# Projecting the mLSTM's values with tokens on partitions, two heads at a time

## The chip, the cores and the metric

One core of a Trainium2 chip runs the whole kernel in one launch. TensorE (PE) multiplies matrices, VectorE (DVE), ScalarE (ACT) and GpSimd (POOL) work on elements, and DMA queues move data, issued here by SyncE (SP). The metric is the device time of one execution in microseconds (us): the median of several runs, 1819.1 us for the kernel before.

## The reference, cut to what matters

One layer of a streaming trunk: a prompt of 1024 tokens and eight requests of 16 tokens share the weights, so 1152 token rows go through each product. The layer is a mixer, an attention into 256 memory tokens, and a feed-forward block. The mixer projects the normalised input once, by `w_in`, and splits the columns between four mLSTM heads and four gated-delta (gdn) heads, each 128 wide:

```
proj = xn @ w_in                       # 1024 -> q,k,v,o of 4 mLSTM heads, gates, q,k,v,z of 4 gdn heads
s    = einsum('bhtd,bhsd->bhts', q, k) * w_intra                  # mLSTM: weights within a chunk
num  = w_inter * einsum('bhtk,bhkv->bhtv', q, C0) + einsum('bhts,bhsv->bhtv', s, v)
den  = w_inter * einsum('bhtk,bhk->bht', q, n0) + sum(s, -1)
h    = num / maximum(abs(den), exp(-m))
C1   = decay0 * C0 + einsum('bhs,bhsk,bhsv->bhkv', w_s, k, v)     # the state carried to the next chunk
```

The queries and keys of an mLSTM head enter `s` with features on the contracted axis. Its values `v` enter only sums over tokens (`s @ v`, `k^T v`), where tokens are contracted.

## The kernel before, in words

**Products.** All data is float32. For a projection each operand is split into a high and a low fp32r half (`xh`, `xl`, `wh`, `wl`), and a product is three matmuls (`mm3`, L233 to L235; L234 to L236 in the changed kernel). A projection chunk is one column block of 128 features: for each of three blocks of 384 tokens, eight steps over the 1024 inputs, three matmuls each, so 72 matmuls of 384 columns, with features on the partitions of the result. The weights of a chunk (128x1024) are loaded by SP, cast on ACT (`wh`, L213) and subtracted on DVE (`wl`, L214). DVE moves each result out of PSUM and scales it by the row norm.

**The stream.** `mixers()` lists the chunks in order: first the gates, then for the heads g0 m0 g1 m1 g2 m2 g3 m3 their columns (gdn: k, q, v, which go through a short convolution; mLSTM: k, q, v), and each head's output gate (`z`) two heads late. Behind them stand eight chunks of the memory tokens' keys (`mem_k`) and eight of their values, 256 columns per matmul. A small planner, `Driver`, runs while the program is written: each dense step advances its clock by a modelled TensorE time, and generators (a head's recurrence, `gdn` or `mlstm`, and `mem_in`) are written out among the dense matmuls when their delay has passed and the flags they wait for (`until`, `wait`) are set. A scheduler then may move an instruction by priority. What stands where on each engine is fixed when the kernel is built.

**A gdn head.** `gdn` loads a decay matrix `D` by DMA (L698), transposes keys and queries (`kt`, `qt`, L263) while ACT sums squares (`junk`, L728), adds masks to `D` on POOL (L703, L704), takes exponentials on ACT, and multiplies keys with keys and queries (`kq`, L755 and L756, evacuated by two DVE operations, L757 and L758). A long recurrence follows; its last product with the state is L909. `head_out` multiplies by the norm on POOL (L967, 128x1152), transposes back (`ot`, L263), applies the gate on DVE and stores.

**An mLSTM head.** `mlstm` waits for the gates, its k, q and v and for the head before it. It loads its row `R`, transposes v in nine 128x128 pieces (`vt`, L1007) with an ACT copy per three (L1008), then per token tile multiplies keys with queries (`st`, L1016), takes an exponential, and multiplies on DVE (L1018); per three tiles it transposes and weights the keys (`kt`, L1021). A loop over token tiles then forms states and outputs (`p2`, L1043; `p3`, L1050 and L1052).

**The end of the mixing stage.** `mem_in` loads the memory tokens (`mf`, L1103), splits them to `mh` (ACT, L1109) and `ml` (DVE, L1110), and forms their norms: `st` (L297), a reciprocal root, and `bc` (L284). It starts two chunks ahead of `mem_k`, once nine slots of SBUF are free; `mem_k` is written once the norms are under way.

Of the kernel before, what the change touches and what calls it, by code (L numbers as in the profile page):

```python
# [8 lines left out]
F32 = mybir.dt.float32  # L9
# [104 lines left out]
class Kern:  # L114
    def __init__(self, tc, ctx, A):
        self.tc, self.nc, self.A = tc, tc.nc, A
        mk = lambda **k: ctx.enter_context(tc.tile_pool(**k))
        self.sp = mk(name="slots", bufs=NSLOT)
        self.wp = mk(name="wts", bufs=2)
        self.cp = mk(name="consts", bufs=1)  # L120
        self.dp = mk(name="dram", bufs=1, space=bass.MemoryType.DRAM)
        self.pd = self.pm = self.pf = None
        self.n = 0
        self.live, self.held, self.reserve = 0, 0, 0
        self.dr = Driver()
# [183 lines left out]
    def consts(self):  # L309
# [44 lines left out]
    def norm_in(self, b, s, x):  # L354

        nc, v = self.nc, self.nc.vector
        add = lambda e, i, j: e.tensor_tensor(x(i), x(i), x(j), ALU.add)
        for k in range(KT):
            wc = self.prm[:, P_WMIX + k:P_WMIX + k + 1]
            xh, xl = self.xh[k][:, s], self.xl[k][:, s]  # L360
            nc.scalar.activation(xh, x(k), AF.Copy, scale=wc)
            v.scalar_tensor_tensor(xl, x(k), wc, xh, ALU.mult, ALU.subtract)
            self.done.add(f"x{b}{k}")
            yield 0.0, 0.5
        zero = 0.0
        if b == 0:
            zero = self.cp.tile([P, 1], F32, name="zero")
            v.tensor_scalar(zero, xl[:, 0:1], 0.0, None, ALU.mult)
        for k in range(KT):
            nc.scalar.activation(x(k), x(k), AF.Square, bias=zero)  # L370
            if k % 2:
                with self.hp() if b == 0 else ExitStack():
                    add(v, k - 1, k)
            yield 0.0, 0.4
        with self.hp() if b == 0 else ExitStack():
            add(v, 0, 2)
            add(v, 4, 6)
            add(v, 0, 4)
        self.F(3)
        rs = self.t(self.m1, [P, 3], "rsc", bufs=2)  # L380
        yield from self.col_stats(self.m1, x(0), 3, rs, self.rB[:, s], f"rB{b}", delay=SD if b else 2.5, spread=4.0)

    def act1(self, b):
# [274 lines left out]
    def proj_chunk(self, out, key, name):  # L658
        w = yield
        yield from self.room_s(1)  # L660
        o = self.S([P, SLOT], F32, name)

        def fin():
            out[key] = o
            self.done.add(key)

        yield from self.project(w, lambda b, ps: self.scaled(o, b, ps), fin)

    def gate_chunk(self, out, hd, last):

# [319 lines left out]
    def mlstm(self, h, r):  # L990
        nc, v, A, pool = self.nc, self.nc.vector, self.A, self.m1
        tl = lambda ap, t: ap[:, t * P:(t + 1) * P]
        self.reserve += 2
        yield from self.until("gates", f"mk{h}", f"mq{h}", f"mv{h}")
        if h:
            yield from self.until(f"mls{h - 1}")
        yield from self.room(2)
        self.reserve -= 2
        k, q, vf = r[f"mk{h}"], r[f"mq{h}"], r[f"mv{h}"]
# [5 lines left out]
        vt = vf[:, :NT * 129].rearrange("p (t d) -> p t d", d=129)  # L1005
# [970 lines left out]
    def mixers(self):  # L1976
# [5 lines left out]
        for kind, h in ORDER:  # L1982
# [3 lines left out]
                    put(base + i, self.conv_chunk(c, r))  # L1986
                body = self.gdn(h, r)
            else:
                base, hd = 16 + 4 * h, h
                for i, c in enumerate("kqv"):  # L1990
                    put(base + i, self.proj_chunk(r, f"m{c}{h}", c))
                body = self.mlstm(h, r)
            start.setdefault(len(seq), []).append((body, 1.0))
# [124 lines left out]
def _layout(x_prompt, x_sample, state_mlstm_C, state_mlstm_n, state_mlstm_m, state_gdn_S, state_gdn_conv,  # L2118
# [10 lines left out]
        cols += [s(2056 + 512), s(2056), s(2056 + 1024), s(3592)]  # L2129
    for h in range(4):  # L2130
        s = lambda o: w[:, o + h * P:o + (h + 1) * P]
        cols += [s(512), s(0), s(1024), s(1536)]
    chunk = lambda m: m.reshape(KT, P, m.shape[1] // P, P).transpose(2, 1, 0, 3).reshape(-1, P, 1024)
    prm = np.zeros((P, P_W), f)
    for o, a in ((P_WMIX, norm_mix_w[0]), (P_WX, norm_x_w[0]), (P_WMEM, norm_mem_w[0]), (P_WFFN, norm_ffn_w[0]),
# [16 lines left out]
        "xT": np.ascontiguousarray(fm(x).reshape(P, KT, NB, BW).transpose(2, 0, 1, 3)),  # L2152
        "memT": fm(mem_prompt[0]),
        "wg": np.stack([w[:, o:o + 4] for o in (2048, 2052, 4104, 4108)], 1).reshape(KT, P, 4, 4).transpose(1, 0, 2, 3),
        "win": chunk(np.concatenate(cols, axis=1)),
        "wout": chunk(w_out[0]), "wq": chunk(wq_x[0]), "wk": chunk(wk_x[0]), "wo": chunk(wo_x[0]),
        "wv": wv_x[0].reshape(2, 4, P, 4, 256).transpose(3, 0, 2, 1, 4).reshape(8, P, 1024),
# [52 lines left out]
```

## Time and profile before

| | |
|---|---|
| runs | 1816.95, 1819.1, 1823.02 us (median 1819.1) |
| profiled execution | 1822.32 us, span 1820.5 us |
| mean granted TensorE clock | 0.988 of full speed |
| busy PE, DVE, ACT, POOL | 98%, 69%, 43%, 10% |
| chain that ended last | PE 85%, DVE 7%, DMA 3%, ACT 2%, POOL 2% |

The span is what the profiler saw between the first and the last instruction; the rest of an execution's time lies around it. A busy share close to one says that PE had matmuls in hand nearly all the time, and says nothing of the pace at which they went. A window is a stretch of the span for which each engine's busy time and the granted clock are listed: where PE's busy time falls short of the stretch, PE waited; where the clock stands at 0.50, each matmul took about twice its time. In a timeline the distance from one start to the next gives the pace; the durations printed beside them overlap.

### The profile page before, as it was taken

To read this page: it belongs to the slowest core of one execution; us is meant where nothing else is said; L and a number is where in the kernel's file an instruction comes from. 1 tells how busy PE (TensorE), PEld (TensorE's weight loads), DVE (VectorE), ACT (ScalarE), POOL (GpSimd) and SP (SyncE) were. 2 spreads that over 40 slices of the span, in tenths; PEclk is the share of its full clock that TensorE was granted. 3 is DMA by queue.
4 is the path that set the end of the run, shared out by engine and by line. 5 is a ranking of instruction groups with operands and counts; after the bars stand their busy time and mean duration, and the time that the engine had idled before them with its cause. 6 is when DMAs were issued, how large, how long until landed. Compare 5 with 4: busy or idle time off the path is not lost.

```text
span 1820.5 us, 32863 instructions
## 1 busy us (share of the span) xinstructions
PE 1782.3 (98%) x13007; PEld 1728.1 (95%) x13007; DVE 1253.1 (69%) x2427; ACT 791.0 (43%) x1697; POOL 188.9 (10%) x231
## 2 busy tenths in 40 slices
PE   9999999999999999999999989999999899999997
PEld 8998899998999999988999989999999899999997
DVE  7877656765665668544677786566666888877975
ACT  6334323324315455445664444445444533433433
POOL 1124223122112202020000000000000000000003
PEclk9999999999999999999999989999999999999998
DMA  5111121121122476797154533343334843533413
GB/s 188 48 52 54 63 80 55 69 80 52 52 65 89 151 259 219 251 321 236 59 164 151 185 111 123 138 169 130 138 138 180 304 150 113 184 123 123 143 45 105
DMA packets 102258, 243.97 MB, mean 134 GB/s; under 512 B 24624, under 2 KB 50000, under 8 KB 102104
## 3 DMA queue, kind: packets, MB, share of 16 engines
q1 hardware_dynamic: 101232, 241.14, 39.2%
q8 instruction: 103, 1.69, 0.4%
q10 hardware_dynamic: 872, 0.72, 0.1%
q14 instruction: 51, 0.42, 0.1%
HBM read 183.92 MB, written 57.91 MB: 133 GB/s over the span
## 4 chain that ended last, share of the span: by engine, by line
PE 85%; DVE 7%; DMA 3%; ACT 2%; POOL 2%; issue 1%; SPq 1%; DVEq 0%; ACTq 0%; POOLq 0%
PE d L233 12%; PE d L235 11%; PE d L234 11%; PE Y L233 5%; PE Y L234 5%; PE Y L235 5%; PE Z L233 3%; PE Z L235 3%; PE Z L234 3%; PE X L235 3%; PE X L234 3%; PE X L233 3%; PE U L233 1%; PE U L235 1%; PE U L234 1%
## 5 line engine op out<-in xcount | busy, mean ns | idle before, releaser
L233 PE MATMUL d<-xh,wh 128*128 128x384 f32 x944 | 342.8, 363 | 1.1 <-DVE k L484 0.6
L235 PE MATMUL d<-xh,wl 128*128 128x384 f32 x944 | 321.4, 340 | 0.6 <-DVE wl L214 0.6
L234 PE MATMUL d<-xl,wh 128*128 128x384 f32 x944 | 318.7, 338 | 0.0
L213 ACT CAST wh<-wr 128x1024 fp32r<-128x1024 f32 x120 | 125.9, 1049 | 241.4 <-PE d L234 184.7
L214 DVE TENSOR_TENSOR wl<-wr,wh 128x1024 fp32r<-128x1024 f32 x120 | 148.7, 1239 | 76.7 <-ACT wh L213 76.4
L233 PEld LDWEIGHTS d<-xh,wh 128*128 128x128 f32 x944 | 179.7, 190 | 7.0 <-issue 5.3
L234 PEld LDWEIGHTS d<-xl,wh 128*128 128x128 f32 x944 | 179.8, 190 | 1.6 <-issue 1.4
L235 PEld LDWEIGHTS d<-xh,wl 128*128 128x128 f32 x944 | 178.7, 189 | 1.0 <-DVE wl L214 1.0
L190 ACT CAST wh<-ws 128x512 fp32r<-128x512 f32 (+3 forms) x148 | 76.2, 537 | 131.5 <-PE Y L234 73.8
L190 ACT CAST wh<-wr 128x512 fp32r<-128x512 f32 (+4 forms) x123 | 71.4, 587 | 128.2 <-PE X L234 46.0
L183 POOL TENSOR_TENSOR csy<-cst,nhalf 128x3 f32<-128x3 f32 (+2 forms) x15 | 12.6, 840 | 1005.8 <-DVE cst L276 1005.0
L233 PE MATMUL Y<-xqh,wh 128*128 128x288 f32 x336 | 99.9, 297 | 0.9 <-DVE h L1680 0.9
L191 DVE TENSOR_TENSOR wl<-ws,wh 128x512 fp32r<-128x512 f32 (+3 forms) x148 | 84.6, 585 | 22.3 <-ACT wh L190 22.1
L233 PE MATMUL Y<-hh,wh 128*128 128x288 f32 x336 | 99.2, 296 | 0.7 <-DVE E L1821 0.6
L234 PE MATMUL Y<-xql,wh 128*128 128x288 f32 x336 | 99.7, 297 | 0.0
L234 PE MATMUL Y<-hl,wh 128*128 128x288 f32 x336 | 99.2, 295 | 0.4 <-DVE hl L191 0.4
L235 PE MATMUL Y<-xqh,wl 128*128 128x288 f32 x336 | 99.6, 296 | 0.0
L235 PE MATMUL Y<-hh,wl 128*128 128x288 f32 x336 | 98.7, 295 | 0.1
L191 DVE TENSOR_TENSOR wl<-wr,wh 128x512 fp32r<-128x512 f32 (+4 forms) x123 | 79.0, 647 | 23.8 <-ACT wh L190 23.6
L190 ACT CAST hh<-ht 128x1152 fp32r<-128x1152 f32 x53 | 61.1, 1157 | 67.6 <-DMA ht<-hD 25.6
L191 DVE TENSOR_TENSOR hl<-ht,hh 128x1152 fp32r<-128x1152 f32 x53 | 71.7, 1354 | 10.2 <-ACT hh L190 10.2
L233 PE MATMUL X<-xqh,wh 128*128 128x288 f32 x224 | 66.1, 295 | 2.4 <-ACT h L1685 2.4
(496 smaller groups left out, 5220.8 us busy)
## 6 DMA issues: line engine op xcount, KB each, us to landing
ht<-hD SPq DMA_DIRECT2D x42, 576.0 KB
hD<-h SPq DMA_DIRECT2D x40, 576.0 KB
wr<-wff SPq DMA_DIRECT2D x40, 512.0 KB
wr<-win SPq DMA_DIRECT2D x32, 512.0 KB
wr<-wout SPq DMA_DIRECT2D x24, 512.0 KB
wr<-wq SPq DMA_DIRECT2D x24, 512.0 KB
wr<-wo SPq DMA_DIRECT2D x24, 512.0 KB
wr<-wd SPq DMA_DIRECT2D x32, 384.0 KB
```

Source lines behind the costliest of these rows:

```text
L183: self.nc.gpsimd.tensor_tensor(y, x, self.nhalf[:, 0:n], ALU.pow)
L190: self.nc.scalar.copy(h, x)
L191: self.nc.vector.tensor_tensor(l, x, h, ALU.subtract)
L213: nc.scalar.copy(wh, raw)
L214: (nc.gpsimd if pool else nc.vector).tensor_tensor(wl, raw, wh, ALU.subtract)
L233: mm(ps, lhsT=lh, rhs=rh, start=start, stop=False, skip_group_check=more)
L234: mm(ps, lhsT=lh, rhs=rl, start=False, stop=False, skip_group_check=more)
L235: mm(ps, lhsT=ll, rhs=rh, start=False, stop=stop, skip_group_check=more)
```

## The change

The values' columns leave the list of 128-wide chunks. A new weight array, `wvm`, holds them as 256-wide blocks (two heads side by side). `v_chunk` projects a pair of heads at once: the token tile is the stationary operand and 256 weight columns stream, so the result has tokens on partitions. Nine token tiles of 24 matmuls make 216 matmuls of 256 columns per pair. Its DVE operation scales by the row norm per token, which is now kept for all nine tiles (`rsm`, 128x9), and writes the layout that the head's loop uses. `v_load` fetches and splits the second half of a pair's weights one chunk earlier. The transposes of v and the ACT copies are removed, and `mlstm` starts with gates, k and q and waits for v only ahead of its loop. The chunk of a pair stands behind the k and q of head 0 or of head 2, so heads 1 and 3 have two chunks (k, q) where they had three, and one of the seven that stood between gdn 3's last convolution and the memory tokens' chunks is gone.

```diff
@@ act1
-        rs = self.t(self.m1, [P, 3], "rsc", bufs=2)
+        rs = self.rsm[:, 3 * b:3 * b + 3]
@@ new functions
+    def v_load(self, pair):
+        yield from self.room(3)
+        raw = self.raw_w(self.A["wvm"][2 * pair + 1], True)
+        yield 0.0, 4.0
+        self.vw[pair] = self.split_w(raw, True)
...
+    def v_chunk(self, out, pair):
+        w = yield
+        yield from self.room_s(2)
+        o = [self.S([P, SLOT], F32, "v") for _ in range(2)]
+        vt = [x[:, :NT * 129].rearrange("p (t d) -> p t d", d=129) for x in o]
+        yield from self.wait(f"vw{pair}")
+        ws = w, self.vw[pair]
+        for t0 in range(0, NT, 2):
+            n = min(2, NT - t0)
...
+            ps = self.D()
+            for j in range(n):
+                xs = slice((t0 + j) * P, (t0 + j) * P + P)
+                for k in range(KT):
+                    (wh, wl), c = ws[k // 4], slice(k % 4 * 256, k % 4 * 256 + 256)
+                    self.mm3(ps[:, j * 256:j * 256 + 256], self.xh[k][:, xs], self.xl[k][:, xs], wh[:, c], wl[:, c],
+                             k == 0, k == KT - 1)
...
+                for i in range(2):
+                    self.nc.vector.tensor_tensor(vt[i][:, t0:t0 + n, 0:P], pv[:, :, i],
+                                                 bc(self.rsm[:, t0:t0 + n], [P, n, P], 2), ALU.mult)
...
@@ mlstm
-        yield from self.until("gates", f"mk{h}", f"mq{h}", f"mv{h}")
+        yield from self.until("gates", f"mk{h}", f"mq{h}")
...
-        for g in (2, 1, 0):
-            pv = self.tr3("vt", lambda t: tl(vf, t), g)
-            nc.scalar.copy(vt[:, 3 * g:3 * g + 3, 0:P], pv)
-            yield 0.33, 0.4
-        nc.gpsimd.memset(vt[:, :, P:P + 1], 1.0)
-        yield 0.0, 0.5
...
-        num = vt
+        yield from self.until(f"mv{h}")
+        vt = num = r[f"mv{h}"][:, :NT * 129].rearrange("p (t d) -> p t d", d=129)
+        nc.gpsimd.memset(vt[:, :, P:P + 1], 1.0)
+        yield 0.0, 0.5
@@ mixers
-                base, hd = 16 + 4 * h, h
-                for i, c in enumerate("kqv"):
+                base, hd = 16 + 3 * h, h
+                body = self.mlstm(h, r)
+                for i, c in enumerate("kq"):
                     put(base + i, self.proj_chunk(r, f"m{c}{h}", c))
...
+                if h % 2 == 0:
+                    start.setdefault(len(seq) - 1, []).append((self.v_load(h // 2), 0.0))
+                    start.setdefault(len(seq), []).append((body, 1.0))
+                    seq.append((A["wvm"][h], self.v_chunk(r, h // 2)))
...
```

What this moves can be read from the order in which each engine's instructions are written. In the rows below a name is followed by a number of its buffer; `d` is a projection's result in PSUM.

First place, PE at mLSTM head 0. Before, the last three `st` and the head's first `p` (p2 and p3) stand beside the end of a 384-column chunk:

```order
L235 MATMUL d_1360<-xh_117,wl_1064 128x384
L1016 MATMUL st_1422<-q_890,k_737 128x128
L233 MATMUL d_1360<-xh_118,wh_1063 128x384
L234 MATMUL d_1360<-xl_126,wh_1063 128x384
L235 MATMUL d_1360<-xh_118,wl_1064 128x384
L1016 MATMUL st_1431<-q_890,k_737 128x128
L1016 MATMUL st_1450<-q_890,k_737 128x128
L263 MATMUL kt_1462<-cst,k_737 128x128 x3
L1043 MATMUL p_198_1470<-v_1067,k_737 128x129
L1050 MATMUL p_200_1474<-v_1067,R_1273 128x129
L1043 MATMUL p_202_1479<-v_1067,k_737 128x129
```

In the changed kernel `st` stands between the 256-column matmuls of the v chunk, each behind a pair of gdn 0's `kq`:

```order
L799 MATMUL kq_1144<-up_224 128x128
L800 MATMUL kq_1144<-up_271,up_224 128x128
L1053 MATMUL st_1151<-q_888,k_735 128x128
L234 MATMUL d_1074<-wh_884,xh_115 128x256
L235 MATMUL d_1074<-wl_885,xh_115 128x256
L236 MATMUL d_1074<-wh_884,xl_123 128x256
L799 MATMUL kq_1158<-up_224 128x128
L800 MATMUL kq_1158<-up_271,up_224 128x128
L1053 MATMUL st_1163<-q_888,k_735 128x128
L234 MATMUL d_1074<-wh_951,xh_116 128x256
L235 MATMUL d_1074<-wl_952,xh_116 128x256
L236 MATMUL d_1074<-wh_951,xl_124 128x256
```

The nine `st` have moved ahead into gdn 0's `kq` stretch, and p2 now comes 160 rows behind the last of them, with dense matmuls of the next chunk between.

Second place, DVE where gdn 0's end meets gdn 1's start. `sot` and `soy` are gdn 0's output norm, behind which POOL's product of L967 (L1011 in the changed kernel) may start; `wl` is the weight of the next chunk. Before:

```order
L959 SCALAR_TENSOR_TENSOR xo_2110<-so_1834,xo_2110 128x9
L184 TENSOR_TENSOR sot_2114<-soy_2113 128x9
L185 SCALAR_TENSOR_TENSOR sot_2114<-sot_2114,xo_2110 128x9
L186 SCALAR_TENSOR_TENSOR soy_2113<-sot_2114,soy_2113 128x9
L631 TENSOR_TENSOR up_1978<-d_2120,rB_127 128x384
L214 TENSOR_TENSOR wl_2156<-wr_2153,wh_2155 128x1024
L639 SCALAR_TENSOR_TENSOR y_1979<-up_1978,prm,y_1979 128x1176 x2
L484 TENSOR_TENSOR z_2159<-d_2160,rB_127 128x384
```

In the changed kernel:

```order
L185 TENSOR_TENSOR sot_2209<-soy_2208 128x9
L653 SCALAR_TENSOR_TENSOR up_1950<-up_1950,y_1951 128x128
L186 SCALAR_TENSOR_TENSOR sot_2209<-sot_2209,xo_2205 128x9
L941 TENSOR_TENSOR qm_3294<-up_1950,cst_76 128x256
L187 SCALAR_TENSOR_TENSOR soy_2208<-sot_2209,soy_2208 128x9
L654 SCALAR_TENSOR_TENSOR up_1950<-up_1950,y_1951 128x1024
L633 TENSOR_TENSOR up_2181<-d_2235,rB_128 128x384
L633 TENSOR_TENSOR up_2181<-d_2265,rB_128 128x384
L215 TENSOR_TENSOR wl_2300<-wr_2297,wh_2299 128x1024
L641 SCALAR_TENSOR_TENSOR y_2182<-up_2181,prm,y_2182 128x1176 x2
```

Between `soy` and `wl` stood one evacuation (L631), and now there are three operations, of which L654 is a 128x1024 product of gdn 1's convolution. The dense matmuls between gdn 0's last product and gdn 1's first `kt` are 132 now, and were 81.

Third place, PE where the memory tokens' keys begin. `ot` is a transpose of the last heads' output, `mh` and `ml` are the memory tokens. Before:

```order
L233 MATMUL d_6733<-xh_118,wh_6394 128x384
L234 MATMUL d_6733<-xl_126,wh_6394 128x384
L235 MATMUL d_6733<-xh_118,wl_6395 128x384
L263 MATMUL ot_6779<-cst,v_5731 128x128 x3
L284 MATMUL bc_6785<-cst,mrs 128x128 x2
L233 MATMUL d_6794<-mh_6558,wh_6630 128x256
L234 MATMUL d_6794<-ml_6560,wh_6630 128x256
L235 MATMUL d_6794<-mh_6558,wl_6631 128x256
```

In the changed kernel:

```order
L264 MATMUL ot_6809<-cst,up_5350 128x128 x3
L234 MATMUL d_6774<-xh_119,wh_6194 128x384
L235 MATMUL d_6774<-xl_127,wh_6194 128x384
L236 MATMUL d_6774<-xh_119,wl_6195 128x384
L264 MATMUL ot_6831<-cst,up_5350 128x128 x3
L264 MATMUL ot_6837<-cst,v_4231 128x128 x3
L234 MATMUL d_6884<-mh_6739,wh_6653 128x256
L235 MATMUL d_6884<-ml_6741,wh_6653 128x256
L236 MATMUL d_6884<-mh_6739,wl_6654 128x256
```

The norm's spreading (`bc`) stood ahead of the first `mem_k` matmul, as did `st`; both now stand among the `mem_k` matmuls, `st` behind 43 of them and `bc` behind 57. Between gdn 3's last L909 (L953 now) and the first `mem_k` matmul there are 48 dense matmuls, 12 transposes and 3 small products.

## Rows read from the trace of the kernel before

**Rows 1.** the page: span, busy shares, one group (busy us, mean ns | idle before)
```profile
span 1820.5 us, 32863 instructions
PE 1782.3 (98%) x13007; PEld 1728.1 (95%) x13007; DVE 1253.1 (69%) x2427; ACT 791.0 (43%) x1697; POOL 188.9 (10%) x231
...
L214 DVE TENSOR_TENSOR wl<-wr,wh 128x1024 fp32r<-128x1024 f32 x120 | 148.7, 1239 | 76.7 <-ACT wh L213 76.4
```

**Rows 2.** windows by stage: us, busy of PE, PEld, DVE, ACT, POOL; clock; DMA
```profile
125.00:145.00 20.00, 17.44 (x119) 15.48 (x117) 19.69 (x44) 6.59 (x16) 6.71 (x5) 1.00 0.18 39
...
216.00:500.00 284.00, 281.62 (x2252) 270.85 (x2251) 177.26 (x409) 92.55 (x264) 60.81 (x70) 1.00 0.20 63
...
598.00:622.00 24.00, 24.00 (x148) 23.85 (x147) 16.14 (x37) 12.42 (x28) 7.96 (x19) 1.00 0.43 138
```

**Rows 3.** timeline around gdn 1's start: start, length, engine, line, instruction [idle before]
```profile
192.29 2.12 POOL L967 TENSOR_TENSOR up<-up,soy 128x1152 f32<-128x1152 f32 x1 [0.76 <-ACT wh L213]
192.53 2.96 DVE L214 TENSOR_TENSOR wl<-wr,wh 128x1024 fp32r<-128x1024 f32 x1
...
196.37 0.33 SPq L698 DMA_DIRECT2D D<-rowD  x1
...
201.64 3.39 POOL L704 TENSOR_TENSOR D<-D,cst 128x1024 f32<-128x1024 f32 x1
...
209.00 0.54 PE L263 MATMUL ot<-cst,up 128*128 128x128 f32 x2 [2.29 <-ACT junk L728]
```

**Rows 4.** windows for PE alone: stretch, PE busy, clock, DMA
```profile
209.20:215.90 6.70, 6.05 (x23) 0.50 0.45 140
...
502.80:509.40 6.60, 5.94 (x21) 0.50 0.46 169
```

**Rows 5.** timeline of PE, 384-column projection
```profile
400.03 0.33 PE L234 MATMUL d<-xl,wh 128*128 128x384 f32 x1
...
402.13 0.33 PE L234 MATMUL d<-xl,wh 128*128 128x384 f32 x1
```

**Rows 6.** timeline of PE, 256-column products of the memory tokens
```profile
622.55 0.28 PE L233 MATMUL d<-mh,wh 128*128 128x256 f32 x1
...
644.97 0.28 PE L233 MATMUL d<-wh,mh 128*128 128x256 f32 x1
```

**Rows 7.** timeline of PE, three transposes of v in a projection
```profile
120.41 0.34 PE L235 MATMUL d<-xh,wl 128*128 128x384 f32 x1
120.58 0.49 PE L263 MATMUL vt<-cst,v 128*128 128x128 f32 x3
...
121.08 0.34 PE L234 MATMUL d<-xl,wh 128*128 128x384 f32 x1
```

**Rows 8.** by tile, vt: durations in ns (min/median/max), first and last start
```profile
L263 PE MATMUL vt<-cst,v x36: 270/272/331, 120.6 to 556.9; 128*128 128x128 f32 x36
```

**Rows 9.** waits of PE, 125 to 145 us: total, times, longest
```profile
PE p L1043 <- DVE k L1021: 1.9, 2, 1.0
```

**Rows 10.** timeline of DVE, two rounds of gdn 0's kq
```profile
104.30 0.28 DVE L757 TENSOR_TENSOR up<-kq,D 128x128 f32<-128x128 f32 x1
...
104.89 0.28 DVE L757 TENSOR_TENSOR up<-kq,D 128x128 f32<-128x128 f32 x1
```

**Rows 11.** by tile, st: what DVE does with one
```profile
L1018 DVE TENSOR_TENSOR R<-st,R x36: 272/282/293, 127.4 to 572.2; 128x128 f32<-128x128 f32 x36
```

**Rows 12.** timeline, gdn 2's second mask operation
```profile
347.31 2.46 POOL L704 TENSOR_TENSOR D<-D,cst 128x1024 f32<-128x1024 f32 x1
```

**Rows 13.** waits of PE, 345 to 360 us, gdn 2's start
```profile
PE qt L263 <- ACT junk L728: 0.2, 1, 0.2
```

**Rows 14.** timeline, end of the mixing stage
```profile
598.77 0.27 PE L909 MATMUL p<-W,kd 128*128 128x128 f32 x1
...
614.62 0.48 DVE L1110 SCALAR_TENSOR_TENSOR ml<-mf,prm,mh 128x256 fp32r<-128x256 f32 x1
...
622.11 0.36 PE L233 MATMUL d<-mh,wh 128*128 128x256 f32 x1
```

More of the change, by code (lines that the diff above doesn't have):

```diff
@@ L126, in __init__ @@
         self.done = set()
+        self.vw = {}
         self.wnext, self.raws = None, {}
@@ L335, in consts @@
         self.rsx = self.cp.tile([P, NT], F32, name="rsx")
+        self.rsm = self.cp.tile([P, NT], F32, name="rsm")
         self.mixD = self.dp.tile([P, KT, T], F32, name="mixD")
@@ L667, in proj_chunk @@
         yield from self.project(w, lambda b, ps: self.scaled(o, b, ps), fin)
+    def v_load(self, pair):
[3 more added lines that the diff above has]
+        self.vw[pair] = self.split_w(raw, True)
+        self.F()
+        self.done.add(f"vw{pair}")
+    def v_chunk(self, out, pair):
[7 more added lines that the diff above has]
+            n = min(2, NT - t0)
+            while self.held > 2:
+                yield WAIT
+            ps = self.D()
[5 more added lines that the diff above has]
+                             k == 0, k == KT - 1)
+                    if j < n - 1 or k < KT - 1:
+                        yield 3 * 256 / 2360.0
+            with self.hp():
+                pv = ps[:, :n * 256].rearrange("p (j h d) -> p j h d", h=2, d=P)
+                for i in range(2):
+                    self.nc.vector.tensor_tensor(vt[i][:, t0:t0 + n, 0:P], pv[:, :, i],
+                                                 bc(self.rsm[:, t0:t0 + n], [P, n, P], 2), ALU.mult)
+            yield 3 * 256 / 2360.0
+        self.F(2)
+        for i in range(2):
+            out[f"mv{2 * pair + i}"] = o[i]
+            self.done.add(f"mv{2 * pair + i}")
+        yield BREAK
     def gate_chunk(self, out, hd, last):
@@ L998, in mlstm @@
         self.reserve -= 2
-        k, q, vf = r[f"mk{h}"], r[f"mq{h}"], r[f"mv{h}"]
+        k, q = r[f"mk{h}"], r[f"mq{h}"]
         R = self.row_bcast(h, "R")
@@ L1004, in mlstm @@
         self.mask_rows(R)
-        vt = vf[:, :NT * 129].rearrange("p (t d) -> p t d", d=129)
-        for g in (2, 1, 0):
-            pv = self.tr3("vt", lambda t: tl(vf, t), g)
-            nc.scalar.copy(vt[:, 3 * g:3 * g + 3, 0:P], pv)
-            yield 0.33, 0.4
-        nc.gpsimd.memset(vt[:, :, P:P + 1], 1.0)
-        yield 0.0, 0.5
         kw = k[:, 0:T].rearrange("p (t d) -> p t d", d=P)
@@ L1988, in mixers @@
             else:
-                base, hd = 16 + 4 * h, h
-                for i, c in enumerate("kqv"):
+                base, hd = 16 + 3 * h, h
+                body = self.mlstm(h, r)
+                for i, c in enumerate("kq"):
                     put(base + i, self.proj_chunk(r, f"m{c}{h}", c))
-                body = self.mlstm(h, r)
-            start.setdefault(len(seq), []).append((body, 1.0))
+                base -= 1
+                if h % 2 == 0:
+                    start.setdefault(len(seq) - 1, []).append((self.v_load(h // 2), 0.0))
+                    start.setdefault(len(seq), []).append((body, 1.0))
+                    seq.append((A["wvm"][h], self.v_chunk(r, h // 2)))
+                    body = None
+            if body is not None:
+                start.setdefault(len(seq), []).append((body, 1.0))
             late.append((base + 3, self.gate_chunk(r, hd, (kind, h) == ORDER[-1])))
@@ L2131, in _layout @@
         s = lambda o: w[:, o + h * P:o + (h + 1) * P]
-        cols += [s(512), s(0), s(1024), s(1536)]
+        cols += [s(512), s(0), s(1536)]
     chunk = lambda m: m.reshape(KT, P, m.shape[1] // P, P).transpose(2, 1, 0, 3).reshape(-1, P, 1024)
@@ L2154, in _layout @@
         "wg": np.stack([w[:, o:o + 4] for o in (2048, 2052, 4104, 4108)], 1).reshape(KT, P, 4, 4).transpose(1, 0, 2, 3),
+        "wvm": w[:, 1024:1536].reshape(2, 4, P, 2, 256).transpose(3, 0, 2, 1, 4).reshape(4, P, 1024),
         "win": chunk(np.concatenate(cols, axis=1)),
```

## Prediction

> **What bounds the kernel now.** The page first: PE is busy 98% of a span of 1820.5 us [rows 1], so a part of the change pays when it takes matmul time off PE, removes one of PE's few waits, or keeps its clock up; work taken off DVE or ACT pays nothing unless PE waits for it. The windows by stage come next, because the shares hide where the other 2% are. From 216 to 500 us, three heads of each kind, PE misses only 284 − 281.62 = 2.4 us [rows 2]. It misses 20 − 17.44 = 2.6 us in one stretch of 20 us at the first mLSTM head [rows 2]. At gdn 1's start one wait takes 2.29 us [rows 3] and the clock then stands at 0.50, that is at 1.2 GHz, for 6.7 us [rows 4]. The end of the mixing stage, 598 to 622 us, has no idle time [rows 2]. These are the places that the change touches. Last the timelines, for the pace: starts lie 2.10/12 = 0.175 us apart at 384 columns [rows 5] and 22.42/189 = 0.1186 us apart at 256 [rows 6].
>
> The sum is made against the profiled execution, 1822.3 us; it stands 3.2 us above the median of 1819.1 us, and I take that off at the end.
>
> **A. The projection itself.** Before, v is four chunks of 72 matmuls: 288 × 0.175 = 50.4 us. After, two chunks of 216 matmuls of 256 columns: 432 × 0.1186 = 51.2 us. That is +0.8 us. It is 128-row loads with 256 columns streaming, the shape that the memory tokens' keys have already, so I see no reason for another pace; if it ran as the columns alone say (two thirds of 0.175 us, 0.1167), A would be 0. Range 0 to +1.
>
> The Trainium skill, page "TensorE: Matmul & The Clock Gate", section "Back-to-back issue gap", says that the spacing of matmuls in a stream of loads and matmuls is set by both, so that small matmuls cost more than their columns. The two rows agree in sign: 0.1186 is 1.6% above two thirds of 0.175.
>
> **B. The transposes.** 36 transposes of v go, in twelve groups of three. Among dense matmuls a group costs PE little: L235 at 120.41, the three transposes, then L233, then L234 at 121.08, which is 0.67 us where two steps of 0.175 would take 0.35; so 0.32 us a group [rows 7], and 12 × 0.32 = −3.9 us. The duration printed for one is 272 ns [rows 8], by which it would be 36 × 0.272 = −9.8 us, but durations overlap, and I take the distance between starts. Range −3.9 to −9.8, weight on the first. The twelve ACT copies and the three waits on them lie beside dense work and pay nothing.
>
> The same page, section "Part 4: PE-mode transpose", gives some 275 ns for a 128x128 transpose in a kernel; 272 ns is that number, as a duration. A sum by it would give an estimate of −9.9 us for B. The row of starts decides here: 0.11 us each.
>
> **C. The first mLSTM head.** Its late start leaves `st`, `kt` and the loop with few dense matmuls between, and PE idles 2.6 us in 125 to 145 us [rows 2], of which 1.9 us is `p2` waiting for the keys on DVE [rows 9]. After, the nine `st` lie in gdn 0's `kq` stretch and p2 comes 160 rows later with dense work ahead of it, so this wait goes. What is late next is DVE in that stretch: a `kq` pair keeps it 0.59 us [rows 10], an `st` 0.28 us more [rows 11], 0.87 us a round. A round of three matmuls of 256 columns is 0.36 us and the three small products stand for about 0.6 us (six of the 0.11 us of B, since fp32 products count double in the records), 0.96 us together: DVE just keeps up. If it did not, nine rounds would lose up to 9 × (0.87 − 0.36) = 4.6 us, less the 2.6 removed: +2. Range −2.6 to +2; I take −2.
>
> **D. gdn 1's start.** Before, POOL's multiply at the end of gdn 0 (2.12 us from 192.29) and the weight's `wl` on DVE (2.96 us from 192.53) stand beside each other [rows 3], and `wl` takes 1.24 us on the mean [rows 1]. `D` is asked for at 196.37, the second mask takes 3.39 us from 201.64, and ACT is then late with its squares, so `ot` at 209.00 waits 2.29 us [rows 3]. With the 0.65 us idle that follows and half of 6.7 us lost to the clock, 3.35 [rows 4], this start costs 2.29 + 0.65 + 3.35 = 6.3 us. gdn 2's start has the same instructions with a mask of 2.46 us [rows 12], and PE waits 0.2 us [rows 13]. After, 132 dense matmuls (23 us at 0.175) instead of 81 (14 us) lie between gdn 0's last product and gdn 1's first `kt`, so gdn 0's end no longer meets it. I take gdn 1 to become like gdn 2 with chance 0.8: −5. Range −6.3 to 0. gdn 3's start, with a clock of 0.50 in 502.8 to 509.4 us [rows 4], keeps its order and its loss.
>
> Here a rule speaks against the change: the Trainium skill, page "SBUF — State Buffer", says that GpSimd and a DVE operation with two SBUF inputs lock one shared port pair, and that the loser waits for the whole instruction. The trace agrees as far as it goes: 192.29 + 2.12 + 1.24 = 195.65, and `wl` ended at 195.49. By it the collision is not removed but handed on, to L654, which follows `soy` now; D would still get the 9 us more of dense work, so I leave its value.
>
> **E. The end of the mixing stage.** This is the change's price. Between gdn 3's last product (598.77) and the first `mem_k` matmul (622.11) PE had 23.3 us of work [rows 14], with no idle time [rows 2]. After, the same two instructions have 48 × 0.175 + 12 × 0.11 + 3 × 0.22 = 10.4 us between them, since one chunk of 12.6 us is gone. The chain behind (memory tokens loaded, split, summed, root) needs its time: the last `ml` started 614.62 and took 0.48, 16.3 us behind gdn 3's product [rows 14]. The scheduler has put 22 `mem_k` matmuls ahead of the first that needs that last `ml`, and seven of the next group: 29 × 0.119 = 3.4 us. So PE arrives at 10.4 + 3.4 = 13.8 and waits to 16.3, at least 2.5 us; then `st` follows 19 matmuls on, `bc` 14 more, and the second and third weights must be there, each another short wait. Bounds: 2 us, if DVE and ACT, which have less to do beside it, shorten the chain, and 23.3 − 10.4 = 12.9 us, if `mem_k` can start no earlier than it did. I take 5, near the chain's own row. A wait of this size has been followed by half clock at both places of [rows 4], at a loss of 3.35; I give that a chance of a third, +1.2.
>
> **F. The rest.** Waits in heads 1 to 3 sum to 2.4 us from 216 to 500 [rows 2] and their order shifts against the dense work: 0, ±2.4. The added weights' traffic replaces the same bytes.
>
> Sum: 0.8 − 3.9 − 2 − 5 + 5 + 1.2 = −3.9. From 1822.3 that is 1818.4, and by the median, 3.2 lower, 1815.2; I round up to 1816, because C and D are gains at near their full size.
>
> **Rivals.**
> (a) *PE starves at the memory tokens* (slower). Place: the first `mem_k`; price 12.9 + 3.35 = 16.3 us instead of 6.2. With the other terms that is +6.2: 1825.3. For it: nothing dense is left to fill in behind it, since everything that follows in the stream needs the same norms, and 23.3 us of cover was exactly used. Against it: the rows put the last `ml` 7 us before the first `mem_k`, so much of the 23.3 was slack, and the norms are now asked for behind 57 `mem_k` matmuls. It decides from a loss of about 15 us on.
> (b) *gdn 1's start stays late* (no change). The wait comes from ACT's queue of squares, exponentials and weight casts, and the masks' 3.39 us, not from gdn 0's end. D = 0: 1820 to 1821. For it: gdn 3's start loses its clock too [rows 4], though another head's end lies elsewhere. Against: gdn 2 [rows 13].
> (c) *The tail hides* (faster): the chain shortens because ACT and DVE have less beside it, E is 1 and no dip: 1816 − 5 = 1811, and with a transpose nearer its duration 1807.
> (d) *The v chunk stalls*: DVE keeps 0.87 us per round against PE's 0.36 where `st` and `kq` crowd five PSUM buffers. C = +2: 1820. That the projection is not used as said, a rival of nothing happening, is excluded by the order of PE.
>
> **How the numbers follow.** A difference under 0.3%, some 5.5 us, can't be told from none with this kernel. Chances: my forecast 0.45 (own range 1811 to 1821; below 1813.6 in about a third of it), (a) 0.2 (slower in four of five), (b) 0.1, (c) 0.18, (d) 0.07. Faster by over 0.3%: 0.15 + 0.18 + a little = 0.36. Slower: 0.16 + 0.02 = 0.19. Within: 0.45. The range of 1808 to 1826 reaches into (a) and (c) and leaves some 2 in 10 out.
>
> **What would show it.** A: v's matmuls 0.119 us apart. B: no `vt` of v, PE instructions fewer by 36 and more by 144. C: no wait of `p` for the keys at head 0, and none of `kq` or `st` over 0.3 us in sum. D: no stretch at 0.50 by gdn 1's start, mask about 2.5 us. E: PE waits in the first 60 `mem_k` matmuls, 2 to 13 us in sum, for `ml`, the norm or a weight; and whether a row of clock 0.50 follows. I am wrong if D's stretch stays, if E is over 10 or under 1, or if a new wait over 3 us stands in heads 1 to 3.

## The result and the profile after

The changed kernel is slower: 1830.1 us median (1825.0 to 1834.07) against 1819.7 us, a ratio of 1.0053 with a 95% interval of 1.0044 to 1.0063, or 10 us. That is above the forecast range of 1808 to 1826. The profiled execution is 1834.07 us, the longest of its kernel, 4 us above the median.

The page of the changed kernel first, the lines that answer to [rows 1]:

```profile
span 1832.3 us, 33094 instructions
PE 1780.2 (97%) x13115; PEld 1725.5 (94%) x13115; DVE 1263.1 (69%) x2435; ACT 789.4 (43%) x1685; POOL 185.2 (10%) x233
```

PE is busy 2.1 us less than before, in a span 11.8 us longer, so its idle time grew by 13.9 us, and that is the loss. The 2.1 us don't show the matmul time by itself: busy time is longer where the clock is lower, and the two executions differ in that (mean granted clock 0.989 here, 0.988 before; a thousandth of 1780 us is 1.8 us). The windows by stage say where PE is idle, with the columns of [rows 2]:

```profile
86.00:94.60 8.60, 6.57 (x39) 6.25 (x38) 6.06 (x14) 0.70 (x4) 3.61 (x4) 1.00 0.61 203
94.70:101.50 6.80, 4.12 (x17) 4.05 (x18) 4.10 (x9) 2.83 (x21) 2.00 (x1) 0.50 0.00 0
125.00:145.00 20.00, 18.65 (x145) 18.02 (x143) 14.45 (x40) 2.60 (x7) 3.50 (x5) 1.00 0.19 39
...
145.00:202.00 57.00, 53.57 (x571) 48.46 (x572) 34.19 (x78) 22.22 (x64) 11.55 (x15) 0.97 0.14 45
...
216.00:500.00 284.00, 277.20 (x2288) 265.18 (x2287) 184.38 (x420) 94.98 (x286) 62.16 (x70) 1.00 0.20 64
...
510.00:598.00 88.00, 84.36 (x782) 80.04 (x781) 60.47 (x156) 32.91 (x114) 21.79 (x19) 1.00 0.24 74
...
623.00:642.00 19.00, 15.58 (x123) 14.45 (x121) 15.19 (x32) 11.65 (x22) 1.85 (x14) 1.00 0.45 169
```

The kernel before, in three of these windows:

```profile
86.00:94.60 8.60, 8.60 (x47) 8.29 (x46) 5.14 (x17) 3.26 (x19) 1.98 (x1) 0.80 0.02 4
...
145.00:202.00 57.00, 56.06 (x592) 51.23 (x582) 40.30 (x90) 24.11 (x71) 19.32 (x19) 1.00 0.17 60
...
510.00:598.00 88.00, 87.28 (x814) 82.60 (x813) 53.68 (x156) 27.61 (x83) 18.75 (x20) 1.00 0.23 74
```

From 125 to 145 us PE now misses 1.4 us where it missed 2.6 [rows 2]. The first head's stall is gone, and most of what is left is the start of another wait, `xa` in the list below, in gdn 0's triangular solve. From 145 to 202 us PE misses 3.4 us where it missed 0.9, from 216 to 500 us 6.8 where it missed 2.4 [rows 2], and from 510 to 598 us 3.6 where it missed 0.7; the last two windows now hold gdn 1's and gdn 3's start, with 1.5 us of waits each. New holes stand at 86 to 101.5 us, where the clock is 0.50 in the last 6.8 us and PE works 4.1 of them, and at 623 to 642 us. There is no stretch at 0.50 by gdn 1's start, nor by gdn 3's, where [rows 4] had them; one of 3.3 us stands at 183.4 us instead. The waits of PE from 60 to 700 us give the holes names (total, times, longest):

```profile
PE db L606 <- ACT cols L594: 4.8, 1, 4.8
PE st L1053 <- DVE R L1055: 3.1, 3, 1.6
PE p L953 <- DVE W L950: 3.0, 2, 1.7
PE p L948 <- DVE sot L186: 2.6, 2, 1.4
PE ot L264 <- ACT junk L772: 2.0, 2, 1.0
PE xa L857 <- DVE Y0T L852: 1.8, 1, 1.8
PE d L234 <- ACT mh L1149: 1.2, 1, 1.2
PE p L948 <- DVE Sg L958: 1.1, 1, 1.1
PE kt L264 <- ACT junk L772: 1.0, 2, 0.5
...
PE p L1083 <- POOL v L1065: 0.2, 1, 0.2
```

The largest is `db`, the last step of the gates' chain, on which every head hangs; nothing of the change touches its lines. The profile names ACT as its releaser, but ACT was idle then: it had waited for DVE. The timeline of the changed kernel shows why (start, length, engine):

```profile
86.23 0.33 SPq L742 DMA_DIRECT2D D<-rowD  x1
...
91.44 2.55 POOL L748 TENSOR_TENSOR D<-D,cst 128x1024 f32<-128x1024 f32 x1
...
91.69 2.35 DVE L585 TENSOR_TENSOR gt<-cols,gt 128x36 f32<-128x36 f32 x1
...
94.35 2.35 POOL L748 TENSOR_TENSOR R<-R,cst 128x1024 f32<-128x1024 f32 x1
94.49 2.26 DVE L592 TENSOR_TENSOR gt<-gt 128x36 f32<-128x36 f32 x1
```

Each mask of POOL meets one of the gates' DVE operations on 128x36 numbers. The first starts 0.25 us into POOL's 2.55 us and ends at 94.04, when the mask is done (93.99); the second likewise, at 96.75 with a mask that ends at 96.70. In the kernel before the same operation took 0.20 us:

```profile
79.73 0.37 SPq L698 DMA_DIRECT2D D<-rowD  x1
...
85.60 2.38 POOL L704 TENSOR_TENSOR D<-D,cst 128x1024 f32<-128x1024 f32 x1
...
90.84 0.20 DVE L583 TENSOR_TENSOR gt<-cols,gt 128x36 f32<-128x36 f32 x1
```

There `D` was asked for at 79.73, and its mask was over at 87.98, before this part of the chain came. In the changed kernel SP asks for it at 86.23, behind the store of `ig`, which waited for DVE, and the mask of R, the first mLSTM head's, follows at once, since that head no longer waits for v. This is the Trainium skill's rule that the prediction weighed at gdn 1's start (page "SBUF — State Buffer", section "SBUF: two separate sides": an exclusive lock between a GpSimd operation that reads SBUF and a DVE operation with two SBUF inputs; the loser waits for the whole instruction). The trace agrees with it to 0.05 us, at a place that the prediction does not treat.

The second new wait is inside gdn's recurrence, four times. At 455 us of the changed kernel:

```profile
454.98 1.81 POOL L184 TENSOR_TENSOR soy<-mx,nhalf 128x9 f32<-128x9 f32 x1 [12.70 <-DVE mx L1129]
...
456.82 0.17 DVE L185 TENSOR_TENSOR sot<-soy 128x9 f32<-128x9 f32 x1 [1.62 <-POOL soy L184]
...
457.98 0.34 DVE L950 SCALAR_TENSOR_TENSOR W<-p,cc,up 128x128 f32<-128x128 f32 x1
...
458.38 0.38 PE L953 MATMUL p<-W,kd 128*128 128x128 f32 x1 [1.35 <-DVE W L950]
```

`soy` is the power in the mLSTM's output norm, 1.81 us on POOL. The DVE operation that needs it (L185) stands in DVE's queue ahead of gdn's `W` (L950), so `W` waits for a norm that nobody is in a hurry for, and PE for `W`. In the changed kernel the recurrence and the earlier mLSTM head's end run side by side.

The third is the one forecast, at the memory tokens' keys. From the first of their matmuls to the first of the values' there were 22.9 us before [rows 6, 14], and now 29.2:

```profile
623.88 0.36 PE L234 MATMUL d<-mh,wh 128*128 128x256 f32 x1
...
653.07 0.28 PE L234 MATMUL d<-wh,mh 128*128 128x256 f32 x1
```

The projection itself goes as forecast; the first and the last of 108 neighbouring matmuls of v, 12.69/107 = 0.1186 us apart:

```profile
408.02 0.36 PE L234 MATMUL d<-wh,xh 128*128 128x256 f32 x1
...
420.71 0.28 PE L236 MATMUL d<-wh,xl 128*128 128x256 f32 x1
```

### The profile page after: what moved, and what is told of

Its sections match the earlier page's. It is cut to its first block, busy times and chain, and to the rows that moved or that the text cites. A ratio compares the mean times of both kernels' runs of the same rounds, so it can differ in the third digit from the quotient of the medians.

```text
span 1832.3 us, 33094 instructions
## 1 busy us (share of the span) xinstructions
PE 1780.2 (97%) x13115; PEld 1725.5 (94%) x13115; DVE 1263.1 (69%) x2435; ACT 789.4 (43%) x1685; POOL 185.2 (10%) x233
## 4 chain that ended last, share of the span: by engine, by line
PE 84%; DVE 8%; DMA 3%; ACT 2%; issue 1%; POOL 1%; SPq 0%; DVEq 0%; ACTq 0%; POOLq 0%
PE d L234 11%; PE d L236 11%; PE d L235 11%; PE Y L234 5%; PE Y L235 5%; PE Y L236 5%; PE X L236 3%; PE X L235 3%; PE X L234 3%; PE Z L235 3%; PE Z L234 3%; PE Z L236 3%; DVE B L830 2%; PE U L234 1%; PE U L236 1%
## 5 line engine op out<-in xcount | busy, mean ns | idle before, releaser
L234 PE MATMUL d<-xh,wh 128*128 128x384 f32 x848 | 308.0, 363 | 1.1 <-DVE k L486 0.6
L236 PE MATMUL d<-xh,wl 128*128 128x384 f32 x848 | 288.6, 340 | 0.6 <-DVE wl L215 0.6
L235 PE MATMUL d<-xl,wh 128*128 128x384 f32 x848 | 285.4, 337 | 0.0
L234 PEld LDWEIGHTS d<-xh,wh 128*128 128x128 f32 x848 | 160.4, 189 | 8.2 <-issue 6.5
L235 PEld LDWEIGHTS d<-xl,wh 128*128 128x128 f32 x848 | 160.8, 190 | 1.5 <-issue 1.4
L236 PEld LDWEIGHTS d<-xh,wl 128*128 128x128 f32 x848 | 159.7, 188 | 1.6 <-DVE wl L215 1.0
L191 ACT CAST hh<-ht 128x1152 fp32r<-128x1152 f32 x53 | 61.1, 1157 | 63.9 <-PE Z L235 23.1
```

The costliest lines, as they stand in the source:

```text
L191: self.nc.scalar.copy(h, x)
L234: mm(ps, lhsT=lh, rhs=rh, start=start, stop=False, skip_group_check=more)
L235: mm(ps, lhsT=lh, rhs=rl, start=False, stop=False, skip_group_check=more)
L236: mm(ps, lhsT=ll, rhs=rh, start=False, stop=stop, skip_group_check=more)
```

## The experiments

Ratios are to the kernel before, run on the same chip beside each group. In the conclusions a difference between two ratios is turned to us with 1820 us; one such difference is uncertain by some 2 to 4 us, as the two intervals give it.

| run | edit, on the changed kernel unless said | median us | ratio | 95% interval |
|---|---|---|---|---|
| e1 | mixer waits for v at its start | 1823.8 | 1.0020 | 1.0011 to 1.0028 |
| e2 | norm's small operations on POOL | 1823.3 | 1.0024 | 1.0014 to 1.0034 |
| e3 | store of ig by ACT's queue | 1826.0 | 1.0034 | 1.0022 to 1.0046 |
| e4 | output gates three heads late | 1828.4 | 1.0052 | 1.0035 to 1.0069 |
| e5 | before, early start alone | 1824.6 | 1.0030 | 1.0019 to 1.0041 |
| e6 | before, norm on POOL | 1819.0 | 0.9996 | 0.9986 to 1.0006 |
| e7 | e1, e2 and e3 together | 1818.9 | 0.9988 | 0.9978 to 0.9998 |
| e8 | masks on DVE | 1819.9 | 0.9996 | 0.9986 to 1.0007 |
| e9 | e2 and e8 | 1816.0 | 0.9972 | 0.9960 to 0.9983 |
| e10 | before, masks on DVE | 1815.5 | 0.9971 | 0.9959 to 0.9983 |
| e11 | before, norm on POOL and masks on DVE | 1812.7 | 0.9950 | 0.9937 to 0.9962 |
| e12 | e9 and late gates | 1811.2 | 0.9949 | 0.9936 to 0.9961 |
| e13 | e11 and late gates | 1808.0 | 0.9930 | 0.9918 to 0.9941 |
| e14 | e12 and e1 | 1808.1 | 0.9934 | 0.9919 to 0.9950 |

**e1, the start taken back.**

```diff
-        yield from self.until("gates", f"mk{h}", f"mq{h}")
+        yield from self.until("gates", f"mk{h}", f"mq{h}", f"mv{h}")
```

> The changed kernel, but the mLSTM mixer waits for its values at its start, as before. Theory Q (queues crossing: the loss of 10 us is made of waits that the earlier mixer and the lost chunk put on in-order queues: the gates' small DVE operations held up by POOL's masks, 4.8 us and a longer stretch at half clock; the mLSTM norm's wait for POOL at the head of DVE's queue inside gdn's recurrence, 5 to 7 us; the memory tokens' keys, 4 us): only heads 0 and 2 start later, as v of heads 1 and 3 is there anyhow. The mask of row R leaves the gates' chain, so the wait of db falls from 4.8 to about 2.5, the wait for the norm inside gdn 2 may go; some of head 0's old 2.6 comes back: 1825 to 1829, ratio to before 1.003 to 1.005. Rival S (the early start alone costs it): back to 1818 to 1821. Rival P (the 256-column projection itself is slower than counted): no change, 1830.

1823.8 us, a little better than expected. Waits of PE:

```profile
PE st L1053 <- DVE R L1055: 4.9, 3, 1.9
PE p L948 <- DVE sot L186: 3.8, 3, 1.4
...
PE db L606 <- ACT cols L594: 1.1, 1, 1.1
```

`db` waits 1.1 us and not 4.8: the mask of R is gone from the chain. The waits for `st` are longer than in the changed kernel (4.9 against 3.1). The early start carries some 6 us of the loss (1.0053 − 1.0020), not all of it. Three of the four waits behind the norm, 3.8 us for `sot`, stand here too, so the early start does not bring those.

**e2, the norm taken off DVE.**

```diff
-        sc = self.rsqrt(pool, mx, NT, tag="so")
...
+        g.tensor_tensor(sc, mx, self.nhalf[:, 0:NT], ALU.pow)
+        g.tensor_tensor(sq, sc, sc, ALU.mult)
+        g.tensor_tensor(sq, sq, mx, ALU.mult)
+        g.tensor_scalar(sq, sq, -0.5, 1.5, ALU.mult, ALU.add)
+        g.tensor_tensor(sc, sq, sc, ALU.mult)
```

Here `g` is POOL.

> The changed kernel, but the three small operations behind the mLSTM norm's power are done on POOL instead of DVE, so that DVE's queue no longer stands waiting for POOL there. Theory Q: the PE waits inside gdn's recurrence at the places of 172, 300, 456 and 591 us (1.3, 1.4, 1.5, 1.6 us) shrink to about 0.3 each; the other waits stay: 1824 to 1826.5, ratio to before 1.003. Rivals S and P: the recurrence waits for its own chain of PE and DVE, nothing moves by over 1.5 us: 1829 to 1831.

1823.3 us. The waits of `p` for `sot` and `Sg` are gone from the list, and one wait for `W` is left of two:

```profile
PE p L953 <- DVE W L950: 1.4, 1, 1.4
```

The mechanism is as expected: all four waits behind the norm are gone. The one for `W` that is left, at 178 us, is not one of them; in the changed kernel it stands at 182 us with 1.7 us. The time fell by 5.3 us (1.0053 − 1.0024).

**e3, the load of D set free.**

```diff
-        nc.sync.dma_start(self.rowD[0:4], rm)
+        nc.scalar.dma_start(self.rowD[0:4], rm)
```

> The changed kernel, but the store of the mLSTM rows (ig) is issued from ACT's queue instead of SP's, so that the load of gdn 0's D is not queued behind it on SP. Theory Q: D is asked for at about 80 us instead of 86.2, POOL's mask of D runs near 84 to 87 as in the kernel before and is over when the gates' chain needs DVE; the mask of R may still meet it. The wait of db falls from 4.8 to 0 to 2.5 us, the stretch at half clock that follows it shortens from 6.8 us or goes: 1823 to 1827. Rival: the gates' chain is late by itself and the masks beside it are chance: the wait of db stays at 4 to 5 us and the time at 1830.

1826.0 us. The timeline:

```profile
79.74 0.42 SPq L742 DMA_DIRECT2D D<-rowD  x1
...
85.68 3.46 POOL L748 TENSOR_TENSOR D<-D,cst 128x1024 f32<-128x1024 f32 x1
...
91.87 2.37 POOL L748 TENSOR_TENSOR R<-R,cst 128x1024 f32<-128x1024 f32 x1
91.92 2.38 DVE L584 TENSOR_TENSOR gt<-gt 128x36 f32<-128x36 f32 x1
```

D is asked for at 79.74 and its mask is out of the way by 89.1; the mask of R still meets one operation of the chain for 2.38 us, and `db` waits 2.2 us. Without D's mask it waits 2.6 us less, without R's (e1) 3.7 less.

**e4, dense work put back ahead of the memory tokens' keys.**

```diff
-            if len(late) > 2:
+            if len(late) > 3:
```

> The changed kernel, but the output gates' chunks come three heads late instead of two, which puts one more chunk of dense work behind gdn 3's last convolution (126 dense matmuls between gdn 3's last product and the first of the memory tokens' keys, where the changed kernel has 48 and the kernel before 117). Theory Q: the waits of 4.2 us in the first 60 matmuls of the memory tokens' keys go; the rest of the stage is shifted too, so the sum is less certain: 1823 to 1828. Rival: those waits belong to the weights of the keys and stay, with the time at 1829 to 1831.

1828.4 us, not told apart from the changed kernel. The waits at the memory tokens' keys went, but others came: one `st` now waits 3.6 us at 254 us. By itself inconclusive; e12 repeats it without the masks.

**e5, the early start alone**, on the kernel before.

```diff
-        yield from self.until("gates", f"mk{h}", f"mq{h}", f"mv{h}")
+        yield from self.until("gates", f"mk{h}", f"mq{h}")
...
-        num = vt
+        yield from self.until(f"mv{h}")
+        vf = r[f"mv{h}"]
```

The nine transposes of v and the fill stand behind the last line now, ahead of the loop.

> The kernel before with one part of the change: the mLSTM mixer starts when its gates, keys and queries are there, and transposes v just ahead of its loop; projection and chunks are those of before. Theory Q: the early start by itself does little here, since v stands one chunk behind q and SP still asks for D ahead of the store of ig; the gates' chain and the memory tokens' keys are untouched, and st meets gdn 0's kq as in the changed kernel: 1817 to 1822, ratio 0.998 to 1.002. Rival S (the early start is the loss): 1825 to 1830.

1824.6 us: 5 us slower, and here theory Q was wrong, rival S nearly right. Two waits of the list:

```profile
PE p L1044 <- POOL v L1026: 3.1, 1, 3.1
...
PE ot L263 <- POOL wr L140: 1.8, 1, 1.8
```

POOL is in both. `p` waits for POOL's small fill beside v, which is queued behind other work there. For `ot` the profile names POOL's touch of a weight buffer, but that ended 0.03 us behind POOL's product of gdn 3's norm (L967, 3.36 us), whose result `ot` reads. In this form, with the transposes and the fill ahead of the loop, starting the mixer early does cost by itself, through the queues that it shares. The changed kernel has no such transposes, and its `p` waits 0.2 us for the fill, so e5 does not price the early start there.

**e6, control of e2**, the same edit on the kernel before.

> Control: the kernel before with the mLSTM norm's three small operations on POOL. Theory Q: what this edit won in the changed kernel (6 to 7 us) was the wait inside gdn's recurrence that the change had made; here only 0.4, 0.9 and 1.0 us of such waits are there, so 1817.5 to 1820, ratio 0.998 to 1.000. Rival N (the edit is good in itself, whatever the change did): 1812 to 1814, ratio 0.997.

1819.0 us, no difference told from none. In the changed kernel the same edit gave 5.3 us, so most of that wait was the change's making.

**e7, the edits of e1, e2 and e3 at once.**

> The changed kernel with three edits at once: mixers of heads 0 and 2 start with their values, as before; the store of ig goes by ACT's queue; the mLSTM norm stays on POOL. Theory Q: neither mask meets the gates' chain, so the wait of db is under 1 us with no stretch at half clock behind 95 us, and the norm's waits are gone; what is left are the waits of st in the gdn solve and the 4.2 us at the memory tokens' keys, against the gains of the projection: 1814 to 1819, ratio to before 0.997 to 1.000. If the edits were not separate causes, 1821 to 1824.

1818.9 us: 12 us faster than the changed kernel, at the level of the kernel before. Together the three edits take back the whole of the loss.

**e8, the masks moved to DVE.**

```diff
     def mask_rows(self, x):
-        v = self.nc.gpsimd
+        v = self.nc.vector
```

> The changed kernel, but both masks of every head are added on DVE instead of POOL. Theory Q with POOL and DVE shutting each other out: the gates' small operations take 0.2 us each again and not 2.3, gdn's solve steps (B) no longer take 2.2 us beside the mask of R, and the wait of db falls from 4.8 to under 2.5 us (DVE now does the 1.2 us masks itself, in its own queue); in sum 1824 to 1828. Rival (the operations were late for another reason, their operands): durations of 2 us and the wait of db stay, 1830.

1819.9 us, better than expected: 10 us from one word. The gates' operations on the timeline:

```profile
92.00 0.19 DVE L585 TENSOR_TENSOR gt<-cols,gt 128x36 f32<-128x36 f32 x1
...
92.33 0.20 DVE L592 TENSOR_TENSOR gt<-gt 128x36 f32<-128x36 f32 x1
...
93.20 0.29 PE L606 MATMUL db<-gt,cst 128*128 128x64 f32 x1
```

0.19 and 0.20 us where they took 2.35 and 2.26; `db` starts at 93.20 with no wait, and no stretch at 0.50 lies behind it. This is the test of the lock: the same operations on the same operands, with POOL quiet, and with the masks in DVE's own queue behind them.

**e9, e10, e11, the edits of e2 and e8 on both kernels** (e10 that of e8 alone).

> The changed kernel with masks on DVE and the mLSTM norm's small operations on POOL. Theory Q (two separate causes): the waits at db and behind the norm are both gone, 1819.9 less the 6 us that the norm's edit won: 1812 to 1815, ratio to before 0.995 to 0.997; left are the waits at the memory tokens' keys (about 4 us) and of st. If the two edits remove the same waits: 1818 to 1820.

> Control: the kernel before with masks on DVE. Theory Q: what it won in the changed kernel (10 us) was mostly the collision at the gates that the change had made; here only the wait at gdn 1's start (3.4 us and a stretch of 6.8 us at half clock, another at gdn 3) hangs on POOL's masks, so 1812 to 1818, ratio 0.996 to 0.999. Rival N (masks on DVE are worth the same anywhere): 1809 to 1811.

> The kernel before with both edits, to price the change where POOL's masks and the norm's wait are out of the way. Theory Q: as with masks alone, 1812 to 1818, and the changed kernel with both edits is then 0 to 3 us faster than this: the projection and the transposes give 3 us, the first head 2.6, the memory tokens' keys take 4. Rival: the change is still slower by 4 us or more.

1816.0, 1815.5 and 1812.7 us. The masks are worth 5 us in the kernel before and 10 in the changed one, so 5 of the 10 us are the change's; the norm adds 4 us on either with the masks away, so there it is no longer the change's. With both edits the changed kernel is still 0.0022 or 4 us behind (0.9972 against 0.9950), the wrong side of what I expected. What waits in it:

```profile
PE d L234 <- ACT mh L1155: 1.6, 1, 1.6
...
PE d L234 <- ACT wh L214: 1.0, 1, 1.0
```

The lines for `mh` and `wh` are the memory tokens' keys.

**e12, e13, the late gates of e4 with their control.**

> The changed kernel with both edits, and the output gates three heads late, so that dense work stands behind gdn 3 as before. Theory Q: the 4 us at the memory tokens' keys go; in the run with late gates alone a wait of 3.7 us of st at 250 us came for it, which may stay: 1808 to 1815. Rival: the waits there are only moved, 1813 or more.

> Control for the last run: the kernel before with masks on DVE, the norm on POOL and the output gates three heads late. Here the memory tokens' keys had no wait, so late gates have nothing to win there. Theory Q: 1811 to 1815, so that the changed kernel with the same three edits (1811.2) is 0 to 3 us faster, which is what projection and transposes give. Rival: late gates are good in themselves, 1807 to 1809, and the projection still costs.

1811.2 and 1808.0 us. In e12 PE has no idle time at the keys, which take 23.1 us:

```profile
596.00:624.00 28.00, 28.00 (x209) 27.92 (x208) 18.17 (x34) 12.94 (x21) 1.78 (x14) 1.00 0.42 143
```

```profile
608.63 0.36 PE L234 MATMUL d<-mh,wh 128*128 128x256 f32 x1
...
631.73 0.28 PE L234 MATMUL d<-wh,mh 128*128 128x256 f32 x1
```

So those waits are what too little dense work costs. But late gates gave the kernel before 3.6 us as well, against my expectation; so their gain on e9, 4.2 us, can't be put down to those waits alone, and the changed kernel stays 3.5 us behind its control (0.9949 against 0.9930).

The clock is in these differences. Each run has its mean granted clock, and time multiplied by it is an estimate of the time at full clock. By the mean of this product over a kernel's runs, late gates gave e9 2.8 us (1800.3 to 1797.5) and the kernel before 0.4 (1795.2 to 1794.8), each uncertain by some 2 us. Most of the 3.6 us is then a higher clock (0.9925 in e13, 0.9910 in e11), and not fewer waits.

**e14, the projection alone**, by the edits of e12 and e1.

> The changed kernel with the same three edits, and the mixers of heads 0 and 2 started with their values as before, so that of the change the projection is left. Theory Q: with masks and norm out of the way the start matters little: 1809 to 1813. Rival S (the early start costs 4 to 5 us wherever it stands): 1806 to 1808.

1808.1 us, 0.7 us from e13, not told apart. What was left in e12 was the early start, 2.7 us by the ratios, which can't be told from none, and 4.6 by the estimate at full clock (1797.5 to 1792.9), uncertain by some 2. And projection and transposes, whose gain of 3 us in PE time was the surest part of the sum, give nothing by the ratios. The whole span of PE, first e14's, then e13's, says where it is:

```profile
0.00:1811.70 1811.70, 1778.89 (x13115) 0.99 0.41 135
```

```profile
0.00:1809.70 1809.70, 1775.20 (x13007) 0.99 0.41 135
```

PE is idle for 32.8 us in e14 and for 34.5 in e13, so its waits as a whole have not grown. It is busy for longer, at a lower clock (0.989 against 0.992 in these executions, 0.9913 against 0.9925 on the mean of the six). By the estimate at full clock e14 is 1.9 us faster than e13 (1792.9 against 1794.8), uncertain by about 1.5. So some of the gain is there, and time at half clock hides it. Why e14 has more of that is open.

The largest wait in e14, 2.9 us of `xa`, is put down to DVE, but that operation of DVE had itself waited for a transfer:

```profile
146.04 0.45 DVE L852 STREAM_TRANSPOSE Y0T<-Yd 128x256 f32<-128x256 f32 x1 [2.89 <-DMA Yd<-yD]
```

## Why the prediction was wrong, by its own steps

- **A and B, the matmuls.** Right as counted: 0.1186 us apart, no `vt` of v, and 108 matmuls more, which is 144 less 36. (12 × 0.32 is 3.8 and not 3.9, which changes nothing.) Of the 3.1 us, e14 against e13 shows about 2 at equal clock and none in the ratios; PE's busy time can't show them.
- **C, the first head.** The wait of `p` for the keys is gone (it was 1.9 [rows 9]; the 0.2 us in the list is a wait for POOL's fill), and the stretch's idle time fell by 1.2 us where I took 2, since a wait of `xa` in gdn 0's solve came in its place. The price that I put beside it, and rival (d) with it, stood at head 0; the waits of `st`, 3.1 us in three places, came at the later heads.
- **D, gdn 1's start.** Right in size: no stretch at 0.50, and `kt` and `ot` wait 0.5 + 1.0 us there, so that the start costs 1.5 us where it cost 6.3, a gain of 4.8 against the 5 of the sum. gdn 3's start, said to keep its loss, has the same 1.5 us and lost its stretch at 0.50 too. But the rule that I weighed and set aside ("I leave its value") decided the case elsewhere.
- **E, the memory tokens.** Sized well: 3.4 us of idle time in 623 to 642 us, against 5 with a chance of half clock, which did not come in this execution. (The chance rested on "a wait of this size" at both places of [rows 4]; at the second, gdn 3's start, no wait was over 1.0 us.) Rival (a), starving at this place at 16 us, gave the right sign for the wrong reason: the place lost about what I took.
- **F, the rest, is the step that failed.** "Their order shifts against the dense work: 0, ±2.4" took the heads' waits of before as a bound for those after. PE's idle time at the places that F stands for grew by some 12 us: 4.8 at the gates, 2.5 from 145 to 202 us, and 4.3 in the two later windows without the starts of gdn 1 and 3. The early start moves the mask of R to POOL beside the gates; the mLSTM's norm now falls into gdn's recurrence; and `D`'s load had moved behind the store of `ig` on SP. I read the order at the places where a wait had been, and not where the moved instructions arrive. By e8 against e10 the masks are 5 us of the change's loss, by e2 against e6 the norm some 4 to 5 (with the masks away, e9 against e11, none of it is the change's), and by e1 the early start 6. These overlap and are not to be added up. The early start brings the mask of R; what moved the norm is not shown, since three of its four waits stay in e1.
- **The other side.** The forecast of faster rested on C and D as gains with nothing on the arriving side. Both came, D nearly whole, and were outweighed.
- **The signs.** None of the signs of being wrong that the prediction lists came: D's stretch went, E lies between 1 and 10 us, and no wait in heads 1 to 3 is over 1.7 us. The largest new wait, 4.8 us, stands ahead of head 0, where no sign was set.

What stays open is why the runs of e14 have a lower clock than those of e13, what moved the norm, and why the norm's edit gains 4 us in both kernels once the masks are away.

## What to carry to other kernels

An instruction that is moved earlier has to be priced where it arrives: on each in-order queue, name what stands behind it while it waits, and for POOL, which DVE operations on SBUF run while it does. A long POOL operation can cost little until a serial chain of tiny DVE operations meets it; then each meeting can cost nearly POOL's whole duration (2.35 us of 2.55 here). Dense work between a long chain's start and its first use is a resource: removing a chunk takes it away even if the work was all on PE.

## What the runs showed of the hardware that I had not expected

- An operation of DVE on 128x36 numbers took 2.35 us instead of 0.20 beside POOL's 2.55 us, ending with it; with POOL quiet, 0.19. In all, the masks on POOL rather than DVE cost 5 us in the kernel before and 10 in the changed one, though DVE then does 1.21 us of work for each long one (e8).
- A power of 9 numbers per partition takes 1.81 us on POOL, nearly as long as its product of 1152 (2.11 us at the shortest).
- Half clock at the gates did not simply follow the waits. With the 4.8 us of `db` a stretch of 6.8 us stood at 94.7 us, and e8, without that wait, has none. But the kernel before had some of it from 86 to 94.6 us (0.80 on the mean), where PE was busy throughout, and e9, where `db` does not wait either, stood at 0.57 with PE busy throughout, in a stretch where e8 has 1.00:

```profile
84.00:92.00 8.00, 8.00 (x32) 7.71 (x32) 3.25 (x7) 1.18 (x3) 0.00 (x0) 0.57 0.61 183
```
